# A decoder trunk on one core: TensorE's order in the attention stages kept as written, with a queue for transposes and value products

## The chip, the cores and the metric

The kernel runs on one core of one Trainium2 chip. It is one program, and the metric is the device time of one execution in microseconds (us). The core has TensorE (PE: matmuls, with a separate row PEld for loading their stationary operand), VectorE (DVE), ScalarE (ACT), GpSimd (POOL) and SyncE (SP, which here issues the weight loads). TensorE writes to PSUM, a memory of eight banks; a bank holds 512 float32 values in each of 128 partitions. The other operands lie in SBUF.

## The reference

Two layers of a decoder, 512 tokens of width 1024, all in float32. Cut to what matters:

```python
h = rmsnorm(x, g_mix[l])
dq, dk, dv, c_q, c_kv_kr, xq, gate_logits = jnp.split(h @ w_in[l], split_idx, axis=-1)
y_diff = diff_attention(...) @ w_diff_o[l]            # 8 heads, two causal softmax maps each, subtracted
y_mla  = latent_attention(...) @ w_mla_o[l]           # 8 heads, causal
y_mem  = memory_cross_attention(...) @ w_cross_o[l]   # 4 heads into 256 memory tokens
gates  = jax.nn.sigmoid((gate_logits + b_gate[l]).reshape(B, S, N_BRANCHES, D))
merged = gates[:, :, 0] * y_diff + gates[:, :, 1] * y_mla + gates[:, :, 2] * y_mem
x = x + merged @ w_out[l]
u = rmsnorm(x, g_mlp[l]) @ w_mlp1[l]
x = x + jnp.square(jax.nn.relu(u)) @ w_mlp2[l]
```

Queries and keys of all three attentions are normalised by head, and those of the first two are rotated by position.

## The kernel before

**Precision.** A weight product is made of three fp32r matmuls (`mm3`, line 110): each operand is split into a high part, which ACT writes, and a low part, which DVE makes by subtraction (`split_into`, line 102). A 512 KB piece of weights is loaded by SP into `wraw`, split into `whi` and `wlo`, and used once; up to three split pieces stand ready.

**Items.** A layer is a list of entries, and the program writes them out one after the other. A *gemm item* is an entry with weights. A *gate item* (`gate_item`, line 777) makes 128 columns of a gate for all 512 tokens: 24 matmuls of 512 columns into a `psacc` bank; DVE scales the sum into a gate tile, and ACT takes the tanh. A *y4 item* multiplies an attention's output by its output weights and joins the result with two gates (`y_mix`, lines 788 to 795). The gates of the cross branch lie in the pool `G`, which has one buffer; two gate items are followed by the y4 item that uses both (`gy4`, line 959). A *head chunk* (`head_chunk`, line 567) is two entries that make queries and keys of one differential head, 48 matmuls of 256 columns each. Behind the second entry come, for either half of the tokens, a copy, a square, a sum, POOL's power -0.5, the rotation (lines 576 to 595), four transposes by TensorE into a `pstp` bank (line 599), and their reading: for either of the two maps, three copies by ACT (line 97) and two subtractions by DVE (lines 607 and 608). K and Q of latent attention (`kvb_item`, `qb_item`) end in four groups of four transposes each (`heads_T`, line 480), every group read by one ACT copy (line 100).

**Attention units.** An attention's queries go in blocks of 128, one *unit* each. A unit makes scores (lines 624 and 627, bank `pss`), the mask and the maximum on DVE (lines 631 to 638), the exponentials on ACT (line 641), for differential attention the difference of its two maps (lines 643 to 646); then it transposes the probabilities (line 652 or 668, bank `pstp`), copies them, and multiplies by the values (line 656, or `mm3` into `pso`). Behind the last unit of a differential head its output is copied, normalised and transposed (line 683). In this text d`h`.`q` is unit q of differential head h.

**Order.** PSUM's eight banks are two `psacc`, three `pss`, two `pstp` and one `pso` (line 76). The text writes nine stages a layer. `PLAN` (line 25) names the gemm items of each; `merge` spreads them evenly behind the attention units of that stage (line 987: none, latent heads in two stages, cross, differential heads two by two in four stages, none). In `PLAN`, gx, gc and gd are the gate items of the latent, cross and differential branch (gc with its y4 items), K and Q the latent projections, h and v the head and value chunks, ym the y4 items of the latent branch, and ":3" takes three items. The text is no fixed order: the framework's scheduler plays it through with a time model and puts out a list for each engine, in which a matmul that the model finds ready goes ahead of one that it finds waiting. On the chip each engine works off its list in order.

The lines that set tiles and banks, and the plan:

```python
PLAN = ["gx:1 K0 gx:1 Q0 gx:1 K1 gx:1 Q1", "gx mem", "xq h0 v0", "h1 ym", "v1 h2 gc:5", "h3 v2 h4 gc:3", "h5 v3 h6 gc", "h7 gd:5", "gd"]
...
    pools = {n: pool(n, b) for n, b in (("O", 16), ("X", 8), ("G", 1), ("B", 40), ("scr", 5), ("PT", 4))}
    p_p = pool("P", 3)
    PS = {n: pool("ps_" + n, b, space=bass.MemoryType.PSUM) for n, b in (("acc", 2), ("s", 3), ("tp", 2), ("o", 1))}
```

Of the kernel before, what the change touches and what calls it, by code (L numbers as in the profile page):

```python
# [15 lines left out]
P = 128  # L16
# [8 lines left out]
PLAN = ["gx:1 K0 gx:1 Q0 gx:1 K1 gx:1 Q1", "gx mem", "xq h0 v0", "h1 ym", "v1 h2 gc:5", "h3 v2 h4 gc:3", "h5 v3 h6 gc", "h7 gd:5", "gd"]  # L25
# [11 lines left out]
MAGIC = 12582912.0  # L37

# [23 lines left out]
def tile_trunk(ctx: ExitStack, tc: tile.TileContext, x_t, mem_t, mem_n, pos, ifr, gcol, grow, w_ck, w_cq, w_kvb, w_qb,  # L62
# [11 lines left out]
    pools = {n: pool(n, b) for n, b in (("O", 16), ("X", 8), ("G", 1), ("B", 40), ("scr", 5), ("PT", 4))}  # L74
# [34 lines left out]

    def mm3(o, l, r, first, last, **kw):  # L110
        T.matmul(o, lhsT=l[0], rhs=r[0], start=first, stop=False, **kw)  # L111
        T.matmul(o, lhsT=l[0], rhs=r[1], start=False, stop=False, **kw)  # L112
        T.matmul(o, lhsT=l[1], rhs=r[0], start=False, stop=last, **kw)  # L113
# [123 lines left out]
    def tok_sums(sqs):  # L237
        q = ps("tp")
        for t in range(NT):
            T.matmul(q[:, t:t + 1], lhsT=sqs[:, t * P:(t + 1) * P], rhs=ones, start=True, stop=True)  # L240
        return q

    def row_stats(sqs):
        q = tok_sums(sqs)
        ms = small("ms", 4)
        V.tensor_scalar(ms, q[:, :NT], 1.0 / D, EPS, ALU.mult, ALU.add)
        r = small("r", 4)
        rsq(r, ms, 4)
        q2 = ps("tp")
        for t in range(NT):  # L250
            T.matmul(q2[:, t * P:(t + 1) * P], lhsT=r[:, t:t + 1].broadcast_to([P, P]), rhs=ident, start=True, stop=True)
# [31 lines left out]
    def layer(l):  # L283
        col = lambda c, n=P: gc[:n, l, c:c + 1]
        s = {}
# [57 lines left out]
        def mem_chunk(c):  # L343
            def done(tp, q):
                if c < 2:
# [13 lines left out]
                    tp_ = ps("tp")  # L359
                    for h in range(2):  # L360
                        for t in range(2):
                            T.transpose(tp_[:, h * 256 + t * P:h * 256 + (t + 1) * P], in_=yv[:, t * 2 + h, :], identity=ident)
                    o = tl("B")
                    scale_to(o, tp_, col(C_CK))
                    s["mk"].append(o)
# [11 lines left out]
        def xq_chunk(c):  # L377
            def done(tp, q):
# [15 lines left out]
                tp_ = ps("tp")  # L394
                for h in range(2):
                    for t in range(2):
                        T.transpose(tp_[:, h * 256 + t * P:h * 256 + (t + 1) * P], in_=yv[:, t * 2 + h, :], identity=ident)
                for h in range(2):
                    scale_to(s["xq", c][h][:, tp * 256:(tp + 1) * 256], tp_[:, h * 256:(h + 1) * 256], col(C_CQ))
# [20 lines left out]
        def ck_finish():  # L420
            ctok, ssk = s["ctok"], s["ssk"]
            ckv = []
            for i in range(2):
                tp_ = ps("tp")
                for t in range(NT):
                    T.transpose(tp_[:, t * P:(t + 1) * P], in_=ctok[t][:, i * P:(i + 1) * P], identity=ident)
# [53 lines left out]
        def heads_T(src, dst, gcolumn):  # L480
            for h in range(4):
                tp_ = ps("tp")
                for t in range(NT):
                    T.transpose(tp_[:96, t * P:(t + 1) * P], in_=src[t][:, h * 96:(h + 1) * 96], identity=ident)
                o = tl("B")
                scale_to(o[:96, :], tp_[:96, :], gcolumn)
                dst.append(o)
# [38 lines left out]
        def qb_item(hf):  # L526
            def fn(w):
                qt = []
                for t in range(NT):
# [16 lines left out]
                    rt = sm.tile([P, 128], F32, tag="rt", name=nm("rt"), bufs=2)  # L546
# [20 lines left out]
        def head_chunk(h):  # L567
            def done(tp, q):
# [27 lines left out]
                tp_ = ps("tp")  # L596
                for c in range(2):
                    for t in range(2):
                        T.transpose(tp_[:, c * 256 + t * P:c * 256 + (t + 1) * P], in_=y[:, t * 256 + c * P:t * 256 + (c + 1) * P], identity=ident)
                sl = slice(tp * 256, (tp + 1) * 256)  # L600
                for m in range(2):
                    own, oth = slice(m * 64, (m + 1) * 64), slice((1 - m) * 64, (2 - m) * 64)
                    qs, ks = tp_[own, 0:256], tp_[own, 256:512]
                    copy_to(qh[m][own, sl], qs)
                    copy_to(kk[m][own, sl], ks)
                    copy_to(qh[m][oth, sl], qs)
                    V.tensor_tensor(out=ql[m][own, sl], in0=qs, in1=qh[m][own, sl], op=ALU.subtract)
                    V.tensor_tensor(out=kk[m][oth, sl], in0=ks, in1=kk[m][own, sl], op=ALU.subtract)
            return chunk256(w_d[l, h], x_h, 4, done)

        def scores(N, qk, causal, ssum, diff):
# [9 lines left out]
            if diff:  # L621
                for m in range(2):
                    for i in range(2):
                        T.matmul(sw[m][:, :max(N, 256)], lhsT=qk[m][0][i], rhs=qk[m][1], start=i == 0, stop=i == 1)  # L624
            else:
                for m in range(2):
                    T.matmul(sv[m], lhsT=qk[m][0], rhs=qk[m][1], start=True, stop=True)  # L627
# [21 lines left out]
        def pv_tok(pt, nb, o, vs):  # L649
            tp_ = ps("tp")  # L650
            for j in range(nb):
                T.transpose(tp_[:, j * P:(j + 1) * P], in_=pt[:, 0, j * P:(j + 1) * P], identity=ident)  # L652
            w = tl("PT")
            copy_to(w[:, :nb * P], tp_[:, :nb * P])
            for j in range(nb):
                T.matmul(o, lhsT=w[:, j * P:(j + 1) * P], rhs=vs(j), start=j == 0, stop=j == nb - 1)  # L656
# [7 lines left out]
        def turned(blocks):  # L664
            tp_ = ps("tp")
            n = len(blocks) * P
            for i, b in enumerate(blocks):
                T.transpose(tp_[:, i * P:(i + 1) * P], in_=b, identity=ident)  # L668
# [9 lines left out]
        def o_finish(o, f, ng, gain, key):  # L678
            ov = o.rearrange("p (g d) -> p g d", g=ng)
            V.tensor_tensor(out=ov, in0=ov, in1=f.unsqueeze(2).broadcast_to([P, ng, 512 // ng]), op=ALU.mult)  # L680
            tp_ = ps("tp")
            for t in range(NT):
                T.transpose(tp_[:, t * P:(t + 1) * P], in_=o[:, t * P:(t + 1) * P], identity=ident)
            hi, lo = tl("O", F32R), tl("O", F32R)
            split_scaled(hi, lo, tp_, gain)
            s.setdefault(key, []).append((hi, lo))

        def o_copy():
            c = tl("scr")
            A.activation(out=c, in_=s["co"], func=AF.Copy)  # L690
            return c

        def cross_att(h):
            c, hh = h // 2, h % 2

            def unit(qp):
                def fn(w):
                    if qp == 0:
                        s["co"] = ps("o")
# [4 lines left out]
                    w = turned([pt[:, m, j * P:(j + 1) * P] for j in range(2) for m in range(2)])  # L704
                    for j in range(2):
                        mm3(s["co"][:, qp * 256:(qp + 1) * 256], tuple(z[:, j * 256 + hh * P:j * 256 + (hh + 1) * P] for z in s["mv"][c]), tuple(z[:, j * 256:(j + 1) * 256] for z in w), j == 0, j == 1)
                    if qp == 1:
                        o_split("oc")
# [3 lines left out]
        def mla_att(hp):  # L712
            hf, h0 = hp // 2, (hp % 2) * 2

            def unit(qi):
                def fn(w):
# [9 lines left out]
                    o = ps("o")  # L726
                    ov = o.rearrange("p (m q t) -> p m q t", m=2, q=2)
                    for j in range(qi + 1):
                        g = 1 if j == qi else 0
                        w = turned([x[:, m, j * P:(j + 1) * P] for m in range(2) for x in pair[g:]])  # L730
                        f = (j % 2) * 256 + h0 * 64
# [434 lines left out]
```

## Time and profile before

| | |
|---|---|
| median of 3 runs | 2000.91 us (1999.56 to 2003.78) |
| the profiled execution | 1999.83 us |
| its span | 1998.0 us |
| mean granted clock of TensorE | 0.997 |

The profile is one execution of the program. "Busy" of PE counts a matmul from its start to a modelled end; matmuls overlap, so a busy PE may still lose a little between two of them. A wait is named by what ended it. A line such as L104 can be that of a helper which many places call; the tiles' names tell which place. The prediction shows the lines of the profile that it uses.

### The profile page before, as it was taken

To read this page: it belongs to the slowest core of one execution; us is meant where nothing else is said; L and a number is where in the kernel's file an instruction comes from. 1 tells how busy PE (TensorE), PEld (TensorE's weight loads), DVE (VectorE), ACT (ScalarE), POOL (GpSimd) and SP (SyncE) were. 2 spreads that over 40 slices of the span, in tenths; PEclk is the share of its full clock that TensorE was granted. 3 is DMA by queue.
4 is the path that set the end of the run, shared out by engine and by line. 5 is a ranking of instruction groups with operands and counts; after the bars stand their busy time and mean duration, and the time that the engine had idled before them with its cause. 6 is when DMAs were issued, how large, how long until landed. Compare 5 with 4: busy or idle time off the path is not lost.

```text
span 1998.0 us, 30334 instructions
## 1 busy us (share of the span) xinstructions
PE 1956.1 (98%) x11888; PEld 1739.9 (87%) x11888; DVE 1352.1 (68%) x2431; ACT 1029.5 (52%) x1929; POOL 305.6 (15%) x209
## 2 busy tenths in 40 slices
PE   8999999999999999999999999999899999999999
PEld 7779989888888899999888899988888888999997
DVE  7756677687745866666657667677777458666665
ACT  5666765555533533344456667555555335344332
POOL 0300101111100222222002001011111002222220
PEclk9999999999999999999999999999999999999999
DMA  5233122222224233333432321121222332232232
GB/s 182 69 112 106 64 64 72 67 69 70 74 64 158 64 106 106 97 104 95 132 113 68 119 92 55 64 76 63 64 74 79 101 126 75 96 106 96 95 107 83
DMA packets 54687, 181.20 MB, mean 91 GB/s; under 512 B 6417, under 2 KB 7441, under 8 KB 54545
## 3 DMA queue, kind: packets, MB, share of 16 engines
q1 hardware_dynamic: 51840, 175.66, 27.2%
q10 hardware_dynamic: 2704, 3.62, 0.6%
q8 instruction: 93, 1.52, 0.3%
q14 instruction: 50, 0.40, 0.1%
HBM read 175.06 MB, written 4.19 MB: 90 GB/s over the span
## 4 chain that ended last, share of the span: by engine, by line
PE 90%; DVE 5%; ACT 2%; issue 1%; DMA 1%; ACTq 0%; DVEq 0%
PE psacc L111 20%; PE psacc L112 20%; PE psacc L113 20%; PE pss L113 5%; PE pss L111 5%; PE pss L112 5%; PE pss L627 2%; PE pso L656 2%; PE pss L624 1%; PE pstp L113 1%; PE pstp L112 1%; PE pstp L111 1%; PE pstp L668 1%; DVE wlo L104 1%; PE pstp L652 1%
## 5 line engine op out<-in xcount | busy, mean ns | idle before, releaser
L103 ACT ACTIVATE whi<-wraw 128x1024 fp32r<-128x1024 f32 (+1 forms) x362 | 378.7, 1047 | 522.6 <-PE psacc L112 225.0
L104 DVE TENSOR_TENSOR wlo<-wraw,whi 128x1024 fp32r<-128x1024 f32 (+1 forms) x362 | 444.6, 1228 | 126.1 <-ACT whi L103 124.4
L111 PE MATMUL psacc<-B,whi 128*128 128x512 f32 x1072 | 421.2, 393 | 2.7 <-DVE G L783 2.7
L112 PE MATMUL psacc<-B,whi 128*128 128x512 f32 x1072 | 419.5, 391 | 0.0
L113 PE MATMUL psacc<-B,wlo 128*128 128x512 f32 x1072 | 418.6, 390 | 0.0
L111 PE MATMUL psacc<-whi,B 128*128 128x256 f32 (+3 forms) x1008 | 302.0, 300 | 14.7 <-ACT whi L103 6.9
L112 PE MATMUL psacc<-wlo,B 128*128 128x256 f32 (+3 forms) x1008 | 295.5, 293 | 1.2 <-DVE wlo L104 1.2
L113 PE MATMUL psacc<-whi,B 128*128 128x256 f32 (+3 forms) x1008 | 293.4, 292 | 0.0
L1055 POOL TENSOR_TENSOR wraw<-wraw,wraw 128x1024 f32<-128x1024 f32 x56 | 152.7, 2726 | 572.0 <-DVE wlo L104 501.9
L111 PEld LDWEIGHTS psacc<-B,whi 128*128 128x128 f32 x1072 | 201.6, 188 | 42.9 <-DVE G L783 3.5
L113 PEld LDWEIGHTS psacc<-B,wlo 128*128 128x128 f32 x1072 | 201.4, 188 | 42.2
L112 PEld LDWEIGHTS psacc<-B,whi 128*128 128x128 f32 x1072 | 201.6, 188 | 37.8
L111 PEld LDWEIGHTS psacc<-whi,B 128*128 128x128 f32 x1008 | 192.9, 192 | 22.7 <-ACT whi L103 6.9
L112 PEld LDWEIGHTS psacc<-wlo,B 128*128 128x128 f32 x1008 | 193.1, 192 | 5.0 <-DVE wlo L104 1.5
L113 PEld LDWEIGHTS psacc<-whi,B 128*128 128x128 f32 x1008 | 192.6, 192 | 1.7
L947 DVE TENSOR_TENSOR X<-psacc,X 128x512 f32<-128x512 f32 x128 | 88.3, 690 | 135.3 <-PE psacc L113 135.3
L111 PE MATMUL pss<-O,whi 128*128 128x256 f32 (+1 forms) x528 | 170.2, 323 | 1.6 <-ACT whi L103 0.9
L112 PE MATMUL pss<-O,whi 128*128 128x256 f32 (+1 forms) x528 | 170.3, 322 | 0.0
L113 PE MATMUL pss<-O,wlo 128*128 128x256 f32 (+1 forms) x528 | 169.7, 323 | 0.3 <-DVE wlo L104 0.3
L136 POOL TENSOR_TENSOR f<-e,mhalf 128x8 f32<-128x8 f32 (+1 forms) x60 | 89.3, 1488 | 469.2 <-DVE e L583 270.3
L641 ACT ACTIVATE P<-pss,nmx 128x128 f32<-128x128 f32 (+2 forms) x224 | 115.4, 521 | 47.9 <-DVE nmx L638 35.7
L111 PEld LDWEIGHTS pss<-O,whi 128*128 128x128 f32 x528 | 100.4, 190 | 13.2 <-ACT whi L103 3.5
(250 smaller groups left out, 3563.9 us busy)
## 6 DMA issues: line engine op xcount, KB each, us to landing
wraw<-in_w_dram SPq DMA_DIRECT2D x128, 512.0 KB, 3.5
wraw<-in_w_g_dram SPq DMA_DIRECT2D x48, 512.0 KB, 3.5
wraw<-in_w_d_dram SPq DMA_DIRECT2D x48, 512.0 KB, 3.7
wraw<-in_w_mem_dram SPq DMA_DIRECT2D x16, 512.0 KB, 3.7
wraw<-in_w_od_dram SPq DMA_DIRECT2D x16, 512.0 KB, 3.6
wraw<-in_w_out_dram SPq DMA_DIRECT2D x16, 512.0 KB, 3.9
X<-in_x_t_dram SPq DMA_DIRECT2D x16, 256.0 KB, 5.1
wraw<-in_w_xq_dram SPq DMA_DIRECT2D x8, 512.0 KB, 3.7
```

Source lines behind the costliest of these rows:

```text
L103: A.activation(out=hi, in_=src, func=AF.Copy)
L104: V.tensor_tensor(out=lo, in0=src, in1=hi, op=ALU.subtract)
L111: T.matmul(o, lhsT=l[0], rhs=r[0], start=first, stop=False, **kw)
L112: T.matmul(o, lhsT=l[0], rhs=r[1], start=False, stop=False, **kw)
L113: T.matmul(o, lhsT=l[1], rhs=r[0], start=False, stop=last, **kw)
L136: G.tensor_tensor(out=o, in0=e, in1=mhalf[:, :n], op=ALU.pow)
L624: T.matmul(sw[m][:, :max(N, 256)], lhsT=qk[m][0][i], rhs=qk[m][1], start=i == 0, stop=i == 1)
L627: T.matmul(sv[m], lhsT=qk[m][0], rhs=qk[m][1], start=True, stop=True)
L641: A.activation(out=pt[:, m, :N], in_=sv[m], func=AF.Exp, bias=nmx[:, m:m + 1], accum_out=ssum[m])
L656: T.matmul(o, lhsT=w[:, j * P:(j + 1) * P], rhs=vs(j), start=j == 0, stop=j == nb - 1)
L947: V.tensor_tensor(out=xt, in0=q, in1=xt, op=ALU.add)
L1055: G.tensor_tensor(out=d["t"], in0=src[0]["t"], in1=src[1]["t"], op=ALU.subtract)
```

## The change

Four things change together.

1. **The order is kept.** All matmuls and transposes go through `mm` and `turn_block`. From the first entry behind the latent projections' inputs to the last gate item (`pinned`), each is marked to stay in program order on TensorE. The other engines' lists are still the scheduler's.
2. **A queue.** Transposes and value products are not written where they arise, but put in a list (`later`) with a due time on a clock that adds up TensorE's estimated work. Transposes of projected heads fall due 12 us on, those of probabilities 9, of a finished head 8, value products 3 us behind their transposes. At each attention unit (or each item, in a stage without units), a *tick*, what is due is written out: value products of latent and cross attention, transposes up to two banks, value products of differential attention, then one more bank of transposes, and the unit's scores; in latent and cross stages the scores come ahead of the last bank.
3. **The plan.** Head chunks are made a stage ahead of their use and stand apart in it.
4. **Tiles.** `G` has two buffers, and `rt`, a scratch tile of the Q projection, one in place of two.

```diff
-PLAN = ["gx:1 K0 gx:1 Q0 gx:1 K1 gx:1 Q1", "gx mem", "xq h0 v0", "h1 ym", "v1 h2 gc:5", "h3 v2 h4 gc:3", "h5 v3 h6 gc", "h7 gd:5", "gd"]
+PLAN = ["gx:1 K0 gx:1 Q0 gx:1 K1 gx:1 Q1", "gx mem", "xq h0 v0", "h1 v1 ym", "h2 gc:3 h3", "v2 h4 gc:3 h5", "v3 h6 gc:3 h7", "gc:3 gd:4", "gd"]
...
-    pools = {n: pool(n, b) for n, b in (("O", 16), ("X", 8), ("G", 1), ("B", 40), ("scr", 5), ("PT", 4))}
+    pools = {n: pool(n, b) for n, b in (("O", 16), ("X", 8), ("G", 2), ("B", 40), ("scr", 5), ("PT", 4))}
...
+    def mm(o, lhsT, rhs, start, stop, **kw):
+        n = math.prod(o.shape[1:])
+        clock[0] += (n / 2.4 + 13.0 if lhsT.dtype == F32R else max(n / 1.2, 108.0)) * 1e-3
+        x = T.matmul(o, lhsT=lhsT, rhs=rhs, start=start, stop=stop, **kw)
+        if pinned[0]:
+            tc.keep_in_program_order(x)
+
+    def turn_block(o, in_):
+        clock[0] += 0.109
+        x = T.transpose(o, in_=in_, identity=ident)
+        if pinned[0]:
+            tc.keep_in_program_order(x)
...
+        def later(lead, kind, banks, fn, since=None, free=lambda: True):
+            seq[0] += 1
+            pend.append((clock[0] + lead, seq[0] if since is None else since, kind, banks, fn, free))
+            return seq[0]
+
+        def due(kind):
+            x = sorted((x for x in pend if x[2] == kind and x[0] <= clock[0]), key=lambda x: x[1])
+            return x[0] if x and x[0][5]() else None
+
+        def run(kind, banks=99):
+            used = 0
+            while True:
+                x = due(kind)
+                if x is None or used + x[3] > banks:
+                    return
+                used += x[3]
+                pend.remove(x)
+                x[4]()
+
+        def ticking(x, plain):
+            fn = x.fn
+
+            def both(w):
+                run(VALUE)
+                run(TURN, 2)
+                run(PLAIN)
+                if plain:
+                    fn(w)
+                run(TURN, 1)
+                if not plain:
+                    fn(w)
+            x.fn = both
...
-        def pv_tok(pt, nb, o, vs):
-            tp_ = ps("tp")
-            for j in range(nb):
-                T.transpose(tp_[:, j * P:(j + 1) * P], in_=pt[:, 0, j * P:(j + 1) * P], identity=ident)
-            w = tl("PT")
-            copy_to(w[:, :nb * P], tp_[:, :nb * P])
-            for j in range(nb):
-                T.matmul(o, lhsT=w[:, j * P:(j + 1) * P], rhs=vs(j), start=j == 0, stop=j == nb - 1)
+        def pv_tok(pt, nb, o_of, vs, end):
+            def turn():
+                tp_ = ps("tp")
+                for j in range(nb):
+                    turn_block(tp_[:, j * P:(j + 1) * P], pt[:, 0, j * P:(j + 1) * P])
+                w = tl("PT")
+                copy_to(w[:, :nb * P], tp_[:, :nb * P])
+
+                def value():
+                    o = o_of()
+                    for j in range(nb):
+                        mm(o, lhsT=w[:, j * P:(j + 1) * P], rhs=vs(j), start=j == 0, stop=j == nb - 1)
+                    end()
+                later(3, PLAIN, 0, value)
+            later(9, TURN, 1, turn, free=lambda: "o_of" not in s)
...
+        plain = phases[1:4]
+        e += [Entry(lambda w: pinned.__setitem__(0, True))]
         for a, sp in zip(phases, PLAN):
-            e += merge(a, take(sp))
+            g = take(sp)
+            for x in a or g:
+                ticking(x, a in plain)
+            e += merge(a, g)
```

Head chunks, memory keys, cross queries, K and Q (`heads_T`), latent and cross units and finished heads put their transposes off in the same way.

More of the change, by code (lines that the diff above doesn't have):

```diff
@@ L37 @@
 MAGIC = 12582912.0
+TURN, VALUE, PLAIN = range(3)
 class Entry:
@@ L284, in layer, with rest @@
         col = lambda c, n=P: gc[:n, l, c:c + 1]
-        s = {}
+        s = {"ready": set()}
+        pend, seq = [], [0]
+        def later(lead, kind, banks, fn, since=None, free=lambda: True):
[26 more added lines that the diff above has]
+            x.fn = both
+        def rest(w):
+            while pend:
+                clock[0] += 1.0
+                run(VALUE)
+                run(TURN, 1)
+                run(PLAIN)
+            pinned[0] = False
         def build_rope():
@@ L393, in done, with turn @@
                 V.tensor_tensor(out=yv, in0=yv, in1=f[:, :4].unsqueeze(2).broadcast_to([P, 4, 128]), op=ALU.mult)
[L394 to L399, printed above, removed]
+                def turn():
+                    tp_ = ps("tp")
+                    for h in range(2):
+                        for t in range(2):
+                            turn_block(tp_[:, h * 256 + t * P:h * 256 + (t + 1) * P], yv[:, t * 2 + h, :])
+                    for h in range(2):
+                        scale_to(s["xq", c][h][:, tp * 256:(tp + 1) * 256], tp_[:, h * 256:(h + 1) * 256], col(C_CQ))
+                    s["ready"].add(("xq", c, tp))
+                later(12, TURN, 1, turn)
             return chunk256(w_xq[l, c], x_h, 4, done)
@@ L480, in heads_T, with head, turn @@
         def heads_T(src, dst, gcolumn):
-            for h in range(4):
[L482 to L487, printed above, removed]
+            def head(h):
+                def turn():
+                    tp_ = ps("tp")
+                    for t in range(NT):
+                        turn_block(tp_[:96, t * P:(t + 1) * P], src[t][:, h * 96:(h + 1) * 96])
+                    o = tl("B")
+                    scale_to(o[:96, :], tp_[:96, :], gcolumn)
+                    dst.append(o)
+                return turn
+            for h in range(4):
+                later(12, TURN, 1, head(h))
         def kvb_item(hf):
@@ L680, in o_finish, with turn @@
             V.tensor_tensor(out=ov, in0=ov, in1=f.unsqueeze(2).broadcast_to([P, ng, 512 // ng]), op=ALU.mult)
[L681 to L691, printed above, removed]
+            def turn():
+                tp_ = ps("tp")
+                for t in range(NT):
+                    turn_block(tp_[:, t * P:(t + 1) * P], o[:, t * P:(t + 1) * P])
+                hi, lo = tl("O", F32R), tl("O", F32R)
+                split_scaled(hi, lo, tp_, gain)
+                s.setdefault(key, []).append((hi, lo))
+            later(8, TURN, 1, turn)
         def cross_att(h):
@@ L703, in fn, with turn, value @@
                     scaled(pt, 256, cs)
[L704 to L708, printed above, removed]
+                    def turn():
+                        w = turned([pt[:, m, j * P:(j + 1) * P] for j in range(2) for m in range(2)])
+                        def value():
+                            if qp == 0:
+                                s["co"] = ps("o")
+                            for j in range(2):
+                                mm3(s["co"][:, qp * 256:(qp + 1) * 256], tuple(z[:, j * 256 + hh * P:j * 256 + (hh + 1) * P] for z in s["mv"][c]),
+                                    tuple(z[:, j * 256:(j + 1) * 256] for z in w), j == 0, j == 1)
+                            if qp == 1:
+                                o_split("oc")
+                        later(3, VALUE, 0, value)
+                    later(9, TURN, 1, turn, free=lambda: "o_of" not in s)
                 return Entry(fn)
@@ L743, in unit @@
+                    z["seq"] = later(9, TURN, 2, turn((0, 1)), free=lambda: s.get("o_of", z) is z)
                 return Entry(fn)
```

137 lines of the change are left out of this document (82 added, 55 removed).

## The prediction, made before the change was run

> **What bounds the kernel now.** First the page: the head, the busy times and the chain that ended last. Then the table of stretches (busy time of each engine between two moments), the list of waits of TensorE in two stretches, and the timeline around the worst ones.
>
> ```profile
> span 1998.0 us, 30334 instructions
> PE 1956.1 (98%) x11888; PEld 1739.9 (87%) x11888; DVE 1352.1 (68%) x2431; ACT 1029.5 (52%) x1929; POOL 305.6 (15%) x209
> PE 90%; DVE 5%; ACT 2%; issue 1%; DMA 1%; ACTq 0%; DVEq 0%
> ```
>
> TensorE (PE) is the bound: 98% busy and 90% of the chain. No product is added or removed, so only the time in which PE stands can change, and all of it is the 42 us between 1956.1 and 1998.0 and what the modelled ends of matmuls cover. Where is it?
>
> ```profile
> 60.00:100.00 40.00, 37.94 (x199) 31.89 (x197) 28.90 (x78) 28.35 (x59) 11.79 (x7) 1.00 0.23 72
> 100.00:150.00 50.00, 45.33 (x233) 38.08 (x233) 28.20 (x62) 32.58 (x71) 4.84 (x5) 0.93 0.34 112
> 150.00:325.00 175.00, 175.00 (x1258) 162.96 (x1257) 117.95 (x234) 114.23 (x260) 18.09 (x17) 1.00 0.23 76
> 325.00:575.00 250.00, 242.63 (x1544) 217.76 (x1542) 187.22 (x435) 136.49 (x309) 37.37 (x36) 0.99 0.22 72
> 575.00:600.00 25.00, 24.39 (x112) 19.09 (x110) 11.45 (x16) 8.87 (x12) 1.01 (x1) 1.00 0.15 49
> 1050.00:1100.00 50.00, 47.94 (x251) 40.65 (x251) 37.66 (x102) 34.65 (x71) 14.61 (x11) 1.00 0.22 68
> 1312.00:1562.00 250.00, 240.60 (x1535) 215.65 (x1534) 187.88 (x436) 136.63 (x311) 31.67 (x28) 1.00 0.23 72
> 1562.00:1590.00 28.00, 27.39 (x130) 21.82 (x129) 13.11 (x18) 9.03 (x13) 1.01 (x1) 1.00 0.18 57
> ```
>
> The columns are: stretch, length, then busy time (instructions) of PE, PEld, DVE, ACT, POOL, and the granted clock. In layer 0, 60 to 100 holds the K and Q projections, 100 to 150 the memory products, 150 to 325 latent and cross attention (PE full: nothing to win), 325 to 575 differential attention, 575 to 600 its end. The other three rows are layer 1. Differential attention stands idle for 7.4 us in layer 0 and 9.4 us in layer 1, although DVE, the next engine, is busy 75% of it. What ends these waits (total, count, longest; 325 to 600, then the largest of layer 1):
>
> ```profile
> PE psacc L111 <- DVE G L794: 1.5, 2, 1.1
> PE psacc L111 <- ACT B L564: 1.4, 1, 1.4
> PE pstp L599 <- DVE scr L595: 1.1, 1, 1.1
> PE psacc L111 <- DVE G L783: 1.0, 2, 0.5
> PE psacc L111 <- ACT scr L576: 0.6, 2, 0.3
> PE pso L656 <- ACT PT L97: 0.5, 1, 0.5
> PE pss L111 <- ACT whi L103: 0.4, 2, 0.2
> PE pss L624 <- ACT P L641: 0.4, 1, 0.4
> PE pss L624 <- DVE B L608: 0.3, 1, 0.3
> PE pss L113 <- DVE wlo L104: 0.2, 1, 0.2
> ...
> PE pss L624 <- DVE B L608: 2.2, 2, 1.9
> ```
>
> Two kinds stand out. Head chunks are turned (L599) and scored (L624) as soon as they are made, and DVE is not done with them. And the one gate tile G holds up the next gate's sum (L783, L794).
>
> **What goes.** Head chunks now come a stage ahead and are turned at least 12 us of the diff's clock after their sums, and G has two buffers, so both kinds should go. Per layer I take the mean of the visible idle time, 8.4 us. A record hides part of a gap:
>
> ```profile
> 448.75 0.60 PE L599 MATMUL pstp<-ident,scr 128*128 128x128 f32 x4
> ...
> 449.11 0.37 PE L112 MATMUL psacc<-wlo,B 128*128 128x256 f32 x1
> 449.31 0.28 PE L113 MATMUL psacc<-whi,B 128*128 128x256 f32 x1
> ...
> 449.43 0.28 PE L111 MATMUL psacc<-whi,B 128*128 128x256 f32 x1
> ```
>
> A 256-column product starts 0.12 us after the one before it (449.31, 449.43) but shows 0.28 us, so each gap is 0.16 us longer than it looks; the 11 waits of the list outside the end (its three have pss L111 and L113) give 1.8 us, and for gaps too short to show I estimate as much again. Together **12 us a layer** (8.4 to 14). The end, where the products behind differential attention await its last head, gives the visible 0.6 us and three such hidden parts, **1.1**. The K and Q stretch stands idle for 2.06 us in either layer: **2.0**. Removed: 15.1 us a layer. The memory stretch of layer 0 loses 4.7 us and some clock, but its inputs come over ACT's own DMAs and copies, which the change leaves; I count it at zero, with -5 to +5 in the range. Four transposes take 0.44 us (448.75 to 449.31 less one pitch of 0.12) whether grouped or not, so grouping itself costs nothing.
>
> **What comes.** PE's order in these stages is now that of the text. So where a group finds no free bank, all behind it waits: scores, the next weight product. The transposes' banks (ps_tp) are still two, and a tick can issue three groups. How often follows from the diff's own due times: I add up its clock along the plan, from the first entry kept in order. With h.q for unit q of head h, in stage "h2 gc:3 h3" h2's two groups fall due at 256 and 259 us, the group of unit 0.2 at 258. Unit 0.3 ticks at 254, too early; unit 1.0 at 261 finds all three due. It issues both h2 groups, a value product, then the third group, and only then its scores. The same happens at 3.1, 5.1 and 6.2: four times a layer. How long is a bank held?
>
> ```profile
> 449.39 1.03 ACT L97 ACTIVATE B<-pstp 64x256 fp32r<-64x256 f32 x3 [0.34 <-PE pstp L599]
> ...
> 450.53 0.41 DVE L607 TENSOR_TENSOR B<-pstp,B 64x256 fp32r<-64x256 f32 x1
> ...
> 450.95 0.42 DVE L608 TENSOR_TENSOR B<-pstp,B 64x256 fp32r<-64x256 f32 x1
> ...
> 451.46 1.04 ACT L97 ACTIVATE B<-pstp 64x256 fp32r<-64x256 f32 x3 [0.23 <-DVE B L608]
> ...
> 452.92 0.43 DVE L607 TENSOR_TENSOR B<-pstp,B 64x256 fp32r<-64x256 f32 x1
> ...
> 453.36 0.43 DVE L608 TENSOR_TENSOR B<-pstp,B 64x256 fp32r<-64x256 f32 x1
> 453.42 0.38 PE L111 MATMUL psacc<-whi,B 128*128 128x256 f32 x1 [1.43 <-ACT B L564]
> ```
>
> A head group's bank is read by ACT, DVE, ACT, DVE in turn: the second copies wait for DVE's subtraction (the bracket). From the first transpose at 448.75 to the last read at 453.79 it is 5.04 us.
>
> ```profile
> 395.81 0.89 PE pso L656 x8
> ...
> L103 ACT ACTIVATE whi<-wraw 128x1024 fp32r<-128x1024 f32 x348 | 368.1, 1059 | 511.4 <-PE psacc L112 215.3 <-PE pss L112 109.5 <-issue 57.0
> ...
> L100 ACT ACTIVATE B<-pstp,gc 96x512 f32<-96x512 f32 x32 | 20.8, 677 | 2.2 <-PE pstp L484 2.2
> ...
> L690 ACT ACTIVATE scr<-pso 128x512 f32<-128x512 f32 x16 | 9.6, 597 | 28.2 <-PE pso L656 28.1
> ```
>
> (a) The third group reaches PE after two groups (0.88) and a value product of two to four blocks (two records of 0.11 us each: 0.44 to 0.88), 1.3 to 1.8 us in. It waits 5.04 - 1.5 = 3.5 us; without the gaps between the readers 0.3 less, with a weight split (1.06) ahead of them 1 more; if the halves overlapped, 1.4. I take 3.3: **13.2 us a layer** (5.6 to 20).
>
> (b) A wait can also cost clock.
>
> ```profile
> 450.00:455.00 5.00, 3.44 (x26) 3.06 (x25) 4.88 (x14) 3.06 (x9) 2.72 (x3) 0.97 0.07 28
> 455.00:460.00 5.00, 5.00 (x32) 5.00 (x32) 0.95 (x4) 1.53 (x5) 0.00 (x0) 0.69 0.00 0
> ```
>
> After 1.56 us idle the granted clock was 0.69 for 5 us, 1.5 us of PE time lost; the waits of 1.9 us in layer 1 cost none (1.00 there). So 0 to 1.5 each: I take 0.5, **2.0 a layer** (0 to 6). [...]
>
> (c) The one bank of outputs (ps_o): at 2.3 and 3.3 the last value product of one head and the first of the next share a tick, and ACT's copy (0.60, or 1.66 behind a split) lies between: 2 x 1.1 = **2.2**.
>
> (d) K's and Q's head groups come three in a tick four times; the third waits for a copy (0.68, or 1.74 behind a split) less the 0.44 and more of cover: 4 x 0.6 = **2.4** (0.8 to 5).
>
> (e) Six more ticks have three groups with one that is read quickly (0.60): 6 x 0.3 = **1.8** (0 to 4).
>
> Added: 21.6 us a layer; removed 15.1; +6.5, twice +13.0. The profiled execution took 1999.83 us (1998.0 and 1.8 around it), 1.1 below the median of 2000.91, so the sum gives 2012.8, rounded **2013**. What was hidden before, the emptying of banks behind other products, loses its cover; that is the whole mechanism.
>
> **The rivals.** *Faster*: a bank of head values is emptied in 3 us. If ACT reads one half of the partitions while DVE reads the other, the hold is the transposes (0.60), three copies (1.03), then the larger of copies and subtractions (1.04), then 0.85: 3.5 us, and the wait 1.4 to 2.0. The point that decides is whether the wait exceeds some 2 us. With 1.5 us each, no clock lost, and (c) to (e) at 2.5, added is 8.5 a layer: -6.6, twice -13, **1987** (1980 to 1995). For it: nothing in the 150 to 325 row is disturbed by groups today. Against: the bracket after DVE B L608. [...] *Nothing*: bank waits of about 2.3 us repay just what goes, or the pinned order is much like today's: **2000** (1996 to 2004). *Slower still*: stage "h2 gc:3 h3" has two head chunks, and DVE's work for them, where its predecessor "v1 h2 gc:5" has one; DVE falls behind there, and the clock drops at every wait: +13 a layer, **2026**.
>
> **How the numbers follow.** Chances: forecast 0.38 (2004 to 2020), slower still 0.12, nothing 0.18, faster 0.32. A difference below 0.2%, 4 us, can hardly be told from no change. Faster 0.32, same 0.18, slower 0.50. Both signs hold much, so the range reaches from 1982 to 2026, leaving out the far ends of either.
>
> **What would show it.** Right: PE waits at L652 or L683 transposes, or score products, for DVE B L608, four a layer, of 3 us each; waits for G gone; short waits for ACT B L100 behind the K and Q projections. Wrong: 325 to 575 as full as 150 to 325, or the waits there put down to DVE nmx or wlo, which would mean DVE and not the banks; or the memory stretch changing by more than 5 us.

## The result, and the profile after

The changed kernel takes 2113.69 us (median of 4 runs, 2113.12 to 2116.89); the kernel before took 2000.24 us in the runs beside it. The ratio is 1.0572 (95% interval 1.0548 to 1.0595): slower, as forecast, but by 113 us and not by 13. The lines of the profiled execution:

```profile
span 2111.4 us, 30326 instructions
...
PE 1984.9 (94%) x11888; PEld 1767.0 (84%) x11888; DVE 1365.3 (65%) x2431; ACT 1033.6 (49%) x1929; POOL 309.4 (15%) x209
...
PE 85%; ACT 6%; DVE 5%; issue 3%; DMA 1%; POOL 0%; ACTq 0%; DVEq 0%; POOLq 0%
```

TensorE has the same 11888 matmuls. Its idle time, span less busy, is 126.5 us (41.9 before, 84.6 more), and it is busy 28.8 us longer (1956.1 before) with the same work. The mean granted clock is 0.976 (0.997 before). The other engines do as much as before. What ended TensorE's waits, over the whole run (total, count, longest):

```profile
PE pstp L124 <- DVE B L680: 39.9, 10, 4.6
PE pstp L124 <- DVE PT L107: 20.6, 10, 3.0
PE psacc L118 <- ACT O L110: 17.1, 2, 14.1
PE pstp L118 <- DVE scr L535: 8.8, 2, 4.5
PE pstp L124 <- ACT PT L100: 8.7, 6, 1.6
PE psacc L118 <- ACT whi L106: 7.0, 1, 7.0
PE pss L118 <- ACT P L715: 6.5, 2, 3.2
PE pso L118 <- ACT scr L876: 5.3, 4, 1.8
PE pstp L124 <- ACT B L103: 5.1, 6, 1.2
PE psacc L118 <- DVE B L111: 2.0, 3, 1.2
PE psacc L118 <- DVE wlo L107: 1.2, 1, 1.2
PE pss L118 <- DVE scr L1002: 0.7, 2, 0.3
```

Every matmul now has the line of a helper, so the tiles tell the place. `pstp <- DVE B L680` is the forecast wait: a group of transposes for a bank that holds a differential head. The waits for G and for a head chunk's rotation are gone, as forecast. The other large rows are groups behind a latent or cross unit (PT), the memory products (O L110), the sums of the Q projection's squares (scr L535) and scores at a stage boundary (P L715). The first seven rows without that of `whi`, together with those of L876 and L103, make 112.0 of the 126.5 us. By stretch of layer 0, in the columns of the prediction's table:

```profile
60.00:100.00 40.00, 38.65 (x196) 32.80 (x195) 27.81 (x72) 23.37 (x45) 13.12 (x8) 1.00 0.26 77
100.00:150.00 50.00, 34.66 (x171) 27.86 (x170) 23.83 (x55) 28.87 (x60) 4.72 (x5) 0.87 0.34 109
150.00:325.00 175.00, 164.78 (x1156) 151.26 (x1156) 107.80 (x213) 110.56 (x254) 16.43 (x16) 0.98 0.21 68
325.00:575.00 250.00, 219.83 (x1450) 202.60 (x1449) 179.68 (x415) 127.45 (x298) 38.59 (x36) 0.95 0.19 62
```

Differential attention stands idle for 30 us (7.4 before). Latent and cross attention, which was full, stands idle for 10 us, and the memory stretch loses 15 us of idle time and runs at clock 0.87. So the cost is not in differential attention alone. One of the signs of being wrong that the prediction named has come: the memory stretch changed by more than 5 us.

Here is the forecast wait at d1.0, in the timeline of the changed kernel (start, length, work, the wait before it):

```profile
359.95 1.03 PE L124 MATMUL pstp<-ident,scr 128*128 128x128 f32 x8
...
360.82 0.61 PE L118 MATMUL pso<-B,PT 128*128 128x128 f32 x4
360.88 1.01 ACT L100 ACTIVATE B<-pstp 64x256 fp32r<-64x256 f32 x3
...
361.87 1.22 DVE L107 TENSOR_TENSOR wlo<-wraw,whi 128x1024 fp32r<-128x1024 f32 x1
...
363.00 0.41 DVE L679 TENSOR_TENSOR B<-pstp,B 64x256 fp32r<-64x256 f32 x1
...
365.39 0.43 DVE L680 TENSOR_TENSOR B<-pstp,B 64x256 fp32r<-64x256 f32 x1
365.94 0.18 PEld L124 LDWEIGHTS pstp<-ident,P 128*128 128x128 f32 x1 [4.70 <-issue]
365.97 0.45 PE L124 MATMUL pstp<-ident,P 128*128 128x128 f32 x1 [4.54 <-DVE B L680]
```

Both head groups are issued at 359.95, a value product follows, and the third group stands until DVE's read at 365.39 is done. A weight split (L107) goes ahead of the first subtraction, and the reads of the two groups alternate, so the first bank is held for 5.87 us and not 5.04. Behind the third group stand the scores and 24 products of a y4 item, which then run without a wait of their own (366.5 to 373.9).

### The profile page after: what moved, and what is told of

It reads as the page before. It is cut to its first block, busy times and chain, and to the rows that moved or that the text cites. A ratio compares the mean times of both kernels' runs of the same rounds, so it can differ in the third digit from the quotient of the medians.

```text
span 2111.4 us, 30326 instructions
## 1 busy us (share of the span) xinstructions
PE 1984.9 (94%) x11888; PEld 1767.0 (84%) x11888; DVE 1365.3 (65%) x2431; ACT 1033.6 (49%) x1929; POOL 309.4 (15%) x209
## 4 chain that ended last, share of the span: by engine, by line
PE 85%; ACT 6%; DVE 5%; issue 3%; DMA 1%; POOL 0%; ACTq 0%; DVEq 0%; POOLq 0%
PE psacc L118 57%; PE pss L118 18%; PE pstp L118 4%; PE pstp L124 3%; PE pso L118 3%; ACT whi L106 2%; DVE wlo L107 1%; ACT B L100 1%; ACT P L715 1%; DMA B<-in_mem_n_dram 1%; DVE PT L107 0%; DVE B L680 0%; DVE B L679 0%; DVE B L107 0%; DMA gr<-in_grow_dram 0%
## 5 line engine op out<-in xcount | busy, mean ns | idle before, releaser
L118 PE MATMUL psacc<-B,whi 128*128 128x512 f32 x2144 | 668.7, 393 | 0.0
L107 DVE TENSOR_TENSOR wlo<-wraw,whi 128x1024 fp32r<-128x1024 f32 (+1 forms) x362 | 445.3, 1230 | 211.0 <-ACT whi L106 210.4
L118 PE MATMUL psacc<-whi,B 128*128 128x256 f32 (+3 forms) x2016 | 403.7, 295 | 9.0 <-ACT whi L106 7.0
L118 PEld LDWEIGHTS psacc<-whi,B 128*128 128x128 f32 x2016 | 328.3, 194 | 15.1 <-ACT whi L106 7.0
L118 PE MATMUL pss<-O,whi 128*128 128x256 f32 (+1 forms) x1056 | 241.3, 322 | 0.7 <-DVE scr L1002 0.7
L118 PEld LDWEIGHTS pss<-O,whi 128*128 128x128 f32 x1056 | 178.4, 190 | 18.4 <-DVE scr L1002 1.5
L715 ACT ACTIVATE P<-pss,nmx 128x128 f32<-128x128 f32 (+2 forms) x224 | 114.9, 517 | 121.8 <-DVE nmx L712 105.8
L118 PE MATMUL pss<-B,B 128*128 128x256 f32 (+3 forms) x448 | 115.9, 382 | 6.5 <-ACT P L715 6.5
L118 PEld LDWEIGHTS pss<-O,wlo 128*128 128x128 f32 x528 | 100.5, 190 | 7.3
L118 PE MATMUL psacc<-O,whi 128*128 128x512 f32 x256 | 92.1, 445 | 0.0
L124 PE MATMUL pstp<-ident,P 128*128 128x128 f32 x384 | 60.1, 277 | 29.7 <-DVE B L680 22.6
L118 PEld LDWEIGHTS pss<-B,B 128*128 128x128 f32 (+1 forms) x448 | 72.3, 196 | 16.1 <-ACT P L715 8.3
```

The source lines that it names most:

```text
L107: V.tensor_tensor(out=lo, in0=src, in1=hi, op=ALU.subtract)
L118: x = T.matmul(o, lhsT=lhsT, rhs=rhs, start=start, stop=stop, **kw)
L124: x = T.transpose(o, in_=in_, identity=ident)
L715: A.activation(out=pt[:, m, :N], in_=sv[m], func=AF.Exp, bias=nmx[:, m:m + 1], accum_out=ssum[m])
```

## The experiments

Two theories stood against each other. **Theory 1**: the kept order costs the time, because what stands behind a group whose bank is taken cannot go ahead. **Theory 2**: the new plan and order of the text cost it, kept or not. Medians beside one another; idle is span less busy:

| kernel | time, us | PE busy | idle | clock |
|---|---|---|---|---|
| before (profile of the prediction) | 2000.24 | 1956.1 | 41.9 | 0.997 |
| changed | 2113.69 | 1984.9 | 126.5 | 0.976 |
| e1 no kept order | 1964.96 | 1940.9 | 21.9 | 0.997 |
| e2 plan alone | 1987.45 | 1948.4 | 37.2 | 1.000 |
| e3 head copied out | 2054.90 | 1968.3 | 84.8 | 0.985 |
| e4 memory earlier | 2106.90 | 1989.2 | 115.9 | 0.976 |
| e5 kept in differential | 2048.08 | 1964.6 | 81.7 | 0.986 |
| e6 kept until differential | 2028.23 | 1960.4 | 66.0 | 0.987 |
| e7 weight products free | 1977.79 | 1941.7 | 34.3 | 0.995 |
| e8 wait filled | 2110.03 | 1999.8 | 108.4 | 0.981 |
| e9 two groups a tick | 2058.25 | 1970.9 | 85.5 | 0.983 |
| e10 three banks | 2055.62 | 1969.9 | 83.9 | 0.982 |
| e11 free, memory earlier | 1962.71 | 1938.7 | 22.3 | 0.998 |

e1, e2 and e11 are medians of four or five executions (e1 from 1964.43 to 1965.99, e2 from 1986.47 to 1994.54); e3 to e10 are single executions, so a few us between two of them prove nothing.

**e1: the order is not kept.**

```diff
-        e += [Entry(lambda w: pinned.__setitem__(0, True))]
+        e += [Entry(lambda w: pinned.__setitem__(0, False))]
```

> The changed kernel with its queues, plan, two G buffers and single rt, but with the flag that keeps TensorE's instructions in program order never set. Theory 1 (the kept order is the cost: what stands behind a transpose or score group whose bank is not free cannot go ahead): TensorE's waits fall from 125.8 us to about the 45 of the kernel before, its half-clock time from 102 us to some 15, and the time is 1990 to 2015 us. Theory 2 (the plan and the order of the text cost by themselves, pinned or not): 2080 us or more, with waits for DVE B L680 still of 4 us. A time half way, near 2055, would mean that both have a share.

Measured: 1964.96 us, ratio 0.9829 (0.9813 to 0.9846) to the kernel before. That is below both theories' figures: not only does the loss go, but the rest of the change gains 33.5 us (1998.45 for the kernel before in these runs). All that is left of waits of over 1.5 us in the run without a kept order:

```profile
PE psacc L118 <- ACT whi L106: 6.9, 1, 6.9
PE psacc L118 <- ACT O L110: 3.7, 2, 2.5
PE pstp L124 <- DVE PT L107: 2.2, 1, 2.2
PE psacc L118 <- DVE wlo L107: 1.7, 1, 1.7
```

Theory 2 falls. The kept order costs 148.7 us (2113.69 - 1964.96): 104.6 of idle time and 44.0 of longer work. (Without the flag the scheduler may order the other engines' lists in another way too, so this is the price of the kept order with all that follows from it.)

**e2: the kernel before with the new plan, two G buffers and one rt**, no queue and no kept order.

```diff
-PLAN = ["gx:1 K0 gx:1 Q0 gx:1 K1 gx:1 Q1", "gx mem", "xq h0 v0", "h1 ym", "v1 h2 gc:5", "h3 v2 h4 gc:3", "h5 v3 h6 gc", "h7 gd:5", "gd"]
+PLAN = ["gx:1 K0 gx:1 Q0 gx:1 K1 gx:1 Q1", "gx mem", "xq h0 v0", "h1 v1 ym", "h2 gc:3 h3", "v2 h4 gc:3 h5", "v3 h6 gc:3 h7", "gc:3 gd:4", "gd"]
...
-    pools = {n: pool(n, b) for n, b in (("O", 16), ("X", 8), ("G", 1), ("B", 40), ("scr", 5), ("PT", 4))}
+    pools = {n: pool(n, b) for n, b in (("O", 16), ("X", 8), ("G", 2), ("B", 40), ("scr", 5), ("PT", 4))}
...
-                    rt = sm.tile([P, 128], F32, tag="rt", name=nm("rt"), bufs=2)
+                    rt = sm.tile([P, 128], F32, tag="rt", name=nm("rt"), bufs=1)
```

> The kernel before, with only the new plan, the second G buffer and the single rt: no queues, no kept order. Theory 1 (the kept order is the cost): 1990 to 2010 us, waits for G gone, waits of TensorE 40 to 55 us. Theory 2 (the plan is the cost): more than half of the 113 us, so 2060 us or more.

Measured: 1987.45, ratio 0.9951 (0.9933 to 0.9968). The plan, with its tiles, gains 11.0 us of the 33.5 (6 to 13 by the interval); the other 22.5 come from the queue, when the scheduler may still move what stands. Theory 1's expectation was right in kind, but its figures were missed: the time is 2.6 us below its range of 1990 to 2010, and the idle time is 37.2 us where it had waits of 40 to 55. The waits for G are gone.

**e5 and e6: the order kept in one half of the stretch.**

```diff
         for a, sp in zip(phases, PLAN):
+            if a is phases[4]:
+                e += [Entry(lambda w: pinned.__setitem__(0, True))]   # e5; False in e6
```

In e5 the flag is not set ahead of the loop; in e6 it is, as in the change.

> The changed kernel, with TensorE's order kept only from the start of differential attention to the end of its queue (about half of the stretch that was kept). TensorE's waits in that stretch make 74 of the changed kernel's 126 us, where the run without a kept order has almost none. If the two halves of the kept stretch add up, this takes 1965 + 74 + some 20 for clock = 2050 to 2065 us, and its sister (order kept only ahead of differential attention) the rest. Rival (the loss needs the kept order throughout, for what is late at the start is handed on): below 2035 us.

> The changed kernel, with TensorE's order kept only from the K and Q projections to the end of cross attention. If the halves add up: 1965 + 32 of waits + some 15 for clock = 2005 to 2020 us, with the waits for ACT O L110 (14 us), DVE PT L107 (some 20) and DVE scr L535 (8.8) unchanged and none for DVE B L680. Rival: the early waits are made good later by TensorE's other work, so that it takes less than 1990 us.

Measured: 2048.08 and 2028.23, 83.1 and 63.3 us above e1. Together 146.4, against 148.7 for the whole: the halves add up. In e5 I was 2 us under the range; e6 cost 8 us more than I allowed. Its idle time is 44.1 above e1, where I had added 32, although the three waits that I named (14, some 20 and 8.8) make 43 by themselves: that sum was wrong. Its work is 19.5 longer, where I had some 15. Over 40% of the loss thus lies ahead of differential attention, where the prediction's sum had at most 8.4 us ((d) and (e), both layers, at the values taken).

**e7: only attention is kept in order, its weight products are free.**

```diff
+    def mm3w(*a, **kw):
+        was, pinned[0] = pinned[0], False
+        mm3(*a, **kw)
+        pinned[0] = was
```

The items for K, Q, memory, cross queries, values, head chunks, gates and y4 call `mm3w`.

> The changed kernel, in which only attention's own products and transposes are kept in order, and the weight products issued beside them (K, Q, memory, cross queries, values, head chunks, gates) are not. Theory 1 (a wait costs because the weight products queue behind it): these go ahead, TensorE's waits fall below 50 us and the time is 1965 to 1995 us. Rival (attention's chain by itself is slow in this order, so that no filler helps, or the mixed order brings waits of its own): 2050 us or more.

Measured: 1977.79, in theory 1's range. Of the attention waits none is left, and 325 to 590 us is full (265.00 busy of 265.00). So in attention a late bank is harmless as long as weight products can fill the wait; what hurts is the queueing of weight products behind a group that waits. This version is 12.8 us above e1.

```profile
PE psacc L118 <- ACT O L110: 16.6, 2, 13.8
PE psacc L118 <- ACT whi L106: 6.8, 1, 6.8
```

The memory's wait is the exception: it stays at 13.8 us, although the memory's and the gates' products are free here. In e1, where it is 2.5 us, the time before it is filled with attention's own work:

```profile
127.17 1.16 PE L118 MATMUL pso<-PT,B 128*128 128x512 f32 x3
...
139.05 0.58 PE L118 MATMUL psacc<-whi,O 128*128 128x256 f32 x1 [2.51 <-ACT O L110]
```

Between these two lines stand scores, transposes and value products of latent attention; in e7 the value products come only behind the memory's wait. So by these traces the cover that the kept order took away there was attention's own work. Why no gate product filled the wait in e7 was not tested.

**e3, e9, e10: three ways to take away the wait for a head's bank.** e3 empties the bank by one copy, and the six reads use that copy. e9 leaves out the third group in a tick of differential attention. e10 gives transposes three banks and scores two.

```diff
+                    copy_to(y, tp_)      # e3, behind the four transposes
+                    tp_ = y
...
-                run(TURN, 1)             # e9
+                if plain:
+                    run(TURN, 1)
...
-    PS = {n: pool("ps_" + n, b, space=bass.MemoryType.PSUM) for n, b in (("acc", 2), ("s", 3), ("tp", 2), ("o", 1))}   # e10
+    PS = {n: pool("ps_" + n, b, space=bass.MemoryType.PSUM) for n, b in (("acc", 2), ("s", 2), ("tp", 3), ("o", 1))}
```

> The changed kernel, but a head group is copied out of its bank once, and its six reads are made from that copy, so that the bank is held some 1.5 us in place of 5. Theory 1a (the hold of that bank makes the third group wait): the ten waits for DVE B L680 (39.9 us) go or fall below 5 us, half-clock time falls by some 25 to 40 us, and the time is 2045 to 2070 us. Rival (the engines behind are late as a whole, the bank is only where it shows): the wait turns up at the scores or at the copies, and the time stays within 15 us of 2113. The added copies (24 to 32 of some 0.6 us) are on ACT and DVE, which stand idle a third of the time or more.

> The changed kernel, in which a tick of differential attention issues no third group behind its two; that group keeps its place in the queue and goes in the next tick. Theory (the third group, behind two head groups on two banks, is where the order waits): the ten waits for DVE B L680 (39.9 us) fall to those of stage boundaries, at most 8 us, the half clock behind them goes, and the time is 2050 to 2065 us. Rival (the moved group meets the next tick's groups, or its values come late, and the wait only moves): 2095 us or more.

> The changed kernel with three banks for transposes (ps_tp) and two in place of three for scores (ps_s), everything kept in order as before. If the number of banks behind transposes is what makes the kept order wait: the waits for DVE B L680, DVE PT L107 and ACT PT L100 (69 us) go, with some 20 us of half clock, and the time is 2015 to 2035 us. Rival (the scores of one unit take both banks that are left, so the next unit's wait until the exponentials are read): waits for ACT P L715 grow from 6.5 us to 30 or more, and the time stays above 2060 us.

Measured: 2054.90, 2058.25, 2055.62. e3 takes away all ten waits for B L680; idle time falls by 41.7 and TensorE's work by 16.6, so the copy is worth 58.8 us, clock included. (The waits for PT fell by 7.0 us in the same run, and 5.5 us of waits for the copy are new, so 58.8 is near the price of the ten waits, not equal to it.) e9 comes to the same by the other way and leaves 12.3 us of them (I had expected 8 at most). e10 lies between its two theories. The waits for PT are gone and those for B L680 are down to two, but new waits come for the scores' banks (P L715 from 6.5 to 16.2) and, in the products of the MLP that use the same banks, for scr L1002 (from 0.7 to 11.5):

```profile
PE psacc L118 <- ACT O L110: 17.3, 2, 14.6
PE pss L118 <- ACT P L715: 16.2, 11, 3.3
PE pss L118 <- DVE scr L1002: 11.5, 2, 5.8
PE pstp L124 <- DVE B L680: 8.9, 2, 4.4
```

**e4: the memory's statistics ahead of the first kept entry.** In the changed kernel the memory products stood until 149.21. The timeline says why:

```profile
134.19 0.35 ACTq L227 DMA_DIRECT2D B<-in_mem_n_dram  x1
...
137.56 0.63 ACT L228 ACTIVATE B<-B 128x512 f32<-128x512 f32 x1 [0.33 <-DMA B<-in_mem_n_dram]
...
145.63 0.63 ACT L228 ACTIVATE B<-B 128x512 f32<-128x512 f32 x1 [1.93 <-DMA B<-in_mem_n_dram]
145.69 0.82 ACTq L388 DMA_DIRECT2D B<-in_mem_t_dram  x2
...
148.65 0.91 ACT L110 ACTIVATE O<-B,gc 128x256 fp32r<-128x256 f32 x2 [2.30 <-DMA B<-in_mem_t_dram]
...
149.21 0.58 PE L118 MATMUL psacc<-whi,O 128*128 128x256 f32 x1 [14.06 <-ACT O L110]
```

ACT loads a piece, waits for it, squares it, and loads the next, four times (134 to 146 us), before it loads the memory's transposed copy that the products need.

```diff
-        pre = ([Entry(lambda w: mem_stats())] if l == 0 else []) + [Entry(mem_begin)]
+        pre = [Entry(mem_begin)]
...
+        e += [Entry(lambda w: mem_stats())] if l == 0 else []
         e += [Entry(lambda w: pinned.__setitem__(0, True))]
```

> The changed kernel with layer 0's statistics of the memory (loads and squares on ACT) issued ahead of the first pinned entry. Theory 1b (the memory products stand in the kept order and nothing can go ahead of them while ACT makes their input): the wait of 14 us for ACT O L110 shrinks to below 4 us, and of the 17 us at half clock there some 8 us of TensorE time come back: 2090 to 2098 us. Rival (ACT is late there for another reason, its weight splits): the wait stays above 10 us and the time above 2108.

Measured: 2106.90. The waits for ACT O L110 fell from 17.1 to 5.2 us in all, and the long one from 14.1 to 2.8, as theory 1 expected, but the time by 6.8 us in place of 15 or more, outside both ranges: idle time fell by 10.6 us, and TensorE's work became 4.3 us longer. The granted clock rose between 30 and 150 us (0.94 in place of 0.93), was lower after that (0.97 in place of 0.98 from 150 to 300 us, 0.93 in place of 0.98 from 300 to 325), and in the mean stayed at 0.976. The cause of the wait is shown; its whole price is not, by a single run.

**e8: the wait filled with work.** A tick with three groups repeats one transpose of the second head group 28 times.

```diff
+                fill[:] = 28 if sum(x[2] == TURN and x[0] <= clock[0] for x in pend) > 2 else 0, 0
                 run(TURN, 2)
...
+                    for _ in range(fill[0] if fill[1] == 2 else 0):
+                        tc.keep_in_program_order(T.transpose(tp_[:, 384:512], in_=y[:, 384:512], identity=ident))
```

> The changed kernel, in which a tick that issues three groups repeats one transpose of the second head group 28 times (28 x 0.11 = 3.1 us, eight times in the run, so 24.6 us of TensorE work that changes no value). TensorE then stands still 1 to 1.5 us ahead of the third group and not 4 to 4.6. If the idle time brings the half clock behind these waits: half-clock time falls from 102 us to about 70 and the time by 10 to 15 us, to 2098 to 2104, though more work is done. Rival (the half clock has another cause, such as the mixture of work): half-clock time stays within 10 us and the time is 2110 us or more; if the second bank is read later because of the repeats, up to 2125.

Measured: 2110.03. Half-clock time, twice the span by one less the mean clock, is 101 us in the changed kernel and 80 here: neither theory's figure. The time is the rival's (2110 or more). But the places are clear. In the changed kernel, stretches at d1.0 and at a later, shorter wait (length, busy time of PE and of the others, granted clock):

```profile
362.28:365.69 3.41, 0.00 (x0) 0.00 (x0) 3.11 (x7) 3.03 (x10) 0.00 (x0) 1.00 0.44 145
365.69:369.10 3.41, 3.13 (x11) 2.87 (x12) 2.13 (x8) 1.71 (x6) 0.00 (x0) 0.51 0.05 13
...
406.65:410.06 3.41, 1.79 (x17) 1.60 (x15) 1.36 (x2) 2.74 (x5) 0.00 (x0) 1.00 0.02 5
410.06:413.47 3.41, 3.41 (x31) 3.41 (x30) 3.27 (x10) 2.91 (x10) 0.00 (x0) 1.00 0.46 154
```

and the same tick with the wait filled:

```profile
362.50:365.90 3.40, 3.40 (x33) 3.40 (x32) 3.19 (x6) 2.60 (x5) 0.00 (x0) 1.00 0.02 5
365.90:369.30 3.40, 1.92 (x18) 1.76 (x17) 2.06 (x7) 2.34 (x7) 0.00 (x0) 1.00 0.47 154
369.30:372.70 3.40, 3.40 (x18) 2.81 (x16) 2.92 (x11) 2.05 (x8) 0.00 (x0) 1.00 0.00 0
```

A stretch of 3.41 us without work is followed by one at half clock (0.51); with 1.6 us idle (406.65) it is not; and where repeats fill the wait the half clock is gone (1.00 in all three rows). Over the run the half-clock time is 21 us less, which is about six stretches of 3.41 us, and at six of the eight ticks the repeats lay in the wait. At d6.2 they did not, since there the wait is ahead of the second head group, and 6.2 us (2 x 3.1) of the repeats were added to the run. So idle time fell by 18.1, and work grew by 14.9 where 24.6 were put in: 9.7 us of longer matmuls had gone. So it is the idle time that brings the half clock behind these waits. My size for the time was wrong, above all by the repeats that were only added work.

**e11: e1 with the memory's statistics earlier**, placed as in e4.

> The version without a kept order (1965 us), with layer 0's statistics of the memory issued before the K and Q projections. It still waits 8 us between 100 and 150 us, 3.7 of them for ACT O L110. If these hang on ACT's late memory work: 1958 to 1963 us, ratio to the kernel before 0.980 to 0.982. Rival (without a kept order other work fills in already, and the earlier squares put back ACT's weight splits): 1963 to 1970 us, no gain.

Measured: 1962.71, ratio 0.9812 (0.9796 to 0.9829). That is in the first theory's range, but its interval overlaps that of e1, so that it gains on e1 is not shown. Its idle time is not smaller either (22.3 against 21.9): the waits for ACT O L110 fell from 3.7 to 2.5 us, and one of 5.9 us for DVE B L111 is new. Both beat the kernel before and the changed one.

## Why the prediction was wrong in size

The sign was right, with a chance of one half put on it, and so was the mechanism as far as it went: groups wait for the two `pstp` banks, and all behind them waits. What failed is the step that listed and priced the waits. It asked only which groups find no free bank, priced most of those as quickly read, put the late inputs of other products at nothing, and put half a microsecond of clock on a wait. In both layers together, against the visible waits of the changed kernel:

| term | predicted | measured |
|---|---|---|
| removed | 30.2 | 33.5 (e1: all that is not the kept order) |
| (a) group behind two head groups | 26.4, eight waits | 39.9, ten waits |
| (b) clock | 4.0 | some 33 |
| (c) bank of outputs | 4.4 | 5.3 |
| (d) K and Q groups | 4.8 | 5.1 |
| (e) other ticks with three groups | 3.6 | 29.3 (20.6 + 8.7) |
| memory products | 0 (-5 to +5, one layer) | 17.1 |
| sums of squares, stage boundary | not in the sum | 8.8 + 6.5 |

**Removed, (c), (d)** held in size. That e1 gives 33.5 by plan and queue supports the first term as a whole, and not each of its parts: idle time fell by 20.0 us where the prediction had 22.1 of visible idle time, and busy time by 15.2 where it had 8.1 of hidden gaps. That the sum is so near owes something to luck. (d) came in six waits and not eight.

**(a)** came at the four places a layer that the due times gave. At the first three the wait is 4.0 to 4.5 us and not 3.3, near the case "with a weight split ahead of them 1 more", which I had named and not taken. At d6.2 there are two waits a layer, and for one of them I had no term:

```profile
561.90 0.60 PE L124 MATMUL pstp<-ident,scr 128*128 128x128 f32 x4
...
566.55 0.43 DVE L680 TENSOR_TENSOR B<-pstp,B 64x256 fp32r<-64x256 f32 x1
...
567.12 1.08 PE L124 MATMUL pstp<-ident,scr 128*128 128x128 f32 x4 [4.63 <-DVE B L680]
...
572.66 0.30 PE L124 MATMUL pstp<-ident,P 128*128 128x128 f32 x1 [2.75 <-DVE B L680]
```

Here the second head group waits for the last read of the first, and the third group for the last read of the second, although there are two banks: by these waits all three had the same bank. In e10 the two waits left for B L680 (4.4 us each) stand ahead of a third group behind two head groups, although there are three banks. I had counted on banks used alternately. By which rule the scheduler gives out the banks no trace shows.

**(e)** is the bank term that failed most, by a factor of eight. I priced these groups by the ACT copy of 0.60 us, "one that is read quickly". In latent and cross attention a bank of probabilities is read by ACT and then by DVE, which subtracts, and DVE has other work in between:

```profile
237.26 0.82 PE L124 MATMUL pstp<-ident,P 128*128 128x128 f32 x6
...
239.22 0.59 ACT L106 ACTIVATE PT<-pstp 128x512 fp32r<-128x512 f32 x1
...
240.44 0.68 DVE L107 TENSOR_TENSOR PT<-pstp,PT 128x512 fp32r<-128x512 f32 x1
...
241.27 0.63 PE L124 MATMUL pstp<-ident,scr 128*128 128x128 f32 x4 [1.90 <-DVE PT L107]
```

The bank is held from 237.26 to the end of DVE's read at 241.12, 3.86 us. Ten waits are of this kind. Six more, in differential attention, are for a bank that one ACT copy reads, and they take 1.3 to 1.6 us and not 0.3. Together there are 16, not the 12 that I took.

**Memory, sums, stage boundary.** I left the memory products at zero because the change leaves their inputs as they are, and looked for waits only where three groups meet. But every product inside the kept stretch loses its cover, whatever it waits for. The last sentence of my sum says this and was applied to the banks alone. The waits of 14.1, 4.5 and 4.3 stand where an input is late and nothing can pass, and two of 3.2 where scores find their banks not yet read. In e7, where weight products can, those of 4.5, 4.3 and 3.2 are gone; the memory's is not, and what would have covered it is attention's own work, as e1 shows. The row of the memory stretch (clock 0.93, 4.7 us lost) had shown before that its input is late even with a free order.

**(b)** I took 0.5 us for a wait, between a row with 1.5 and one with 0. In the changed kernel the eight waits of over 4 us behind heads, the 4.5 and 4.3 ahead of the sums of squares, and the 14 us of memory wait all brought half clock (0.50) for at least 3.41 us, which costs up to 1.7 us of work (half of 3.41). Adding up how much longer the matmuls at half clock take than the same ones at full clock gives 37 us for the changed kernel, 4 before and 2.5 in e1, an estimate from these three traces. Of the 44.0 us by which the kept order lengthens the work, some 35 are thus clock; what the other 9 are is not shown.

Together: waits of 112 us where I had 39 ((a), (c), (d), (e)), clock 33 where I had 4. Of these 112, some 86 are waits for a bank ((a), (c), (d), (e) and the 6.5 for the scores' banks), and 26 are for late inputs, for which the sum had no term. The rival "slower still" had the right sign. Its first reason, that DVE falls behind, the runs do not bear out: DVE is as busy as before (1365 against 1352 us), and the same DVE work fits beside a full TensorE in e1. Its second, that the clock drops, came true at all eleven waits of over 4 us between matmuls, and at part of the shorter ones.

## What to carry to other kernels

An order that is kept removes the fill behind every wait in it, not only behind those that one thought of. Before TensorE's order is fixed, each input of each product in the stretch has to be known to be early, and each bank's readers have to be counted to the last one, the second engine's too. Here the better part of the change was the queue that puts transposes off: with the scheduler left free to pass what stood, it was worth some 22 us (e2 to e1). What it is worth with the order kept was not run.

## What the runs showed of the hardware

**The half clock stands behind the longer waits.** In the trace of the changed kernel there are 23 stretches at half clock (0.50). Of these 18 last 3.41 us, three twice that and one, at the memory's wait, five times; the last ends with the program. Each of the other 22 starts during an idle time of TensorE of 1.8 us or more between two matmuls, or at most 1.7 us after it:

| idle time between matmuls, us | times | with half clock behind |
|---|---|---|
| 4.0 to 14.1 | 11 | 11 |
| 2.0 to 3.3 | 11 | 9 |
| 1.2 to 1.9 | 15 | 2 |

The length of a wait alone does not tell the shorter ones apart: behind 3.01 us that ended at 1190.15 the granted clock was 0.78 up to 1198, and behind 2.99 us that ended at 261.15 it was 1.00 up to 268. In the kernel before, the prediction's row with 1.56 us idle had a clock of 0.69 behind it.

**Less idle time did not come back in full.** In e4 10.6 us less idle time gave 6.8 us less time. TensorE's work became 4.3 us longer and the mean clock stayed at 0.976, although the wait of 14.1 us had shrunk to 2.8. Why the clock was lower elsewhere (0.93 in place of 0.98 from 300 to 325 us) is not shown.
